# One diffusion-step kernel: the prompt's tile moved to the end of the projection, and three of the first expert's eight first-layer weight blocks multiplied in plain fp32

## The chip, the cores and the metric

One core of a Trainium2 chip runs the whole step. The metric is the device time of one execution in microseconds; before the change it is 2153.65 us, the median of three runs (2150.96 to 2155.9).

## The reference, cut to what matters

128 prompt rows and 1024 latent rows, both 1024 wide, go through one layer. All tensors are fp32.

```
hn   = rmsnorm(x) * (1 + scale1) + shift1            # modulation: silu(c) @ w_mod + b_mod
mix  = (gates * (pooling mixer, bidirectional RG-LRU)(hn @ w_in)) @ w_out
x    = x + gate1 * mix
hn   = rmsnorm(x) * (1 + scale2) + shift2
aff  = softmax(hn @ router_w)                        # 16 experts
gate, idx = top_k(aff over the rows, capacity)       # 128 latent rows and 16 prompt rows per expert
hid  = silu(hn[idx] @ w1) * (hn[idx] @ w3)           # 1024 -> 2048, per expert
y[idx] += (hid @ w2) * gate                          # 2048 -> 1024, per expert
out  = rmsnorm(x + gate2 * y)
```

Prompt and latent rows are routed separately, but an expert multiplies its 128 latent and 16 prompt rows together: 144 columns (`S`). Each expert has 24 MB of weights, so 384 MB are streamed once.

## The kernel before

The order on every engine is written out by hand: the program order of an engine is its issue order. Five stages follow one another.

1. **Start** (`norm1`, `mod_first`, `mod_second`, `hn_first`, `hn_cols`, `hn_low`, `dense_v`, lines 352 to 471). The 1152 rows are normed and transposed into `hn_hi` and `hn_lo`, while the first modulation columns come from 16 blocks `a` of `w_mod`. A matrix product in this kernel is split: a raw fp32 weight block is cast on ScalarE to `hi` (fp32r) and the rest is subtracted on VectorE to `lo` (`split`, lines 181 to 190), and three TensorE products hi·hi, hi·lo, lo·hi follow (`mm3`). Blocks `a` whose number is in `DP` are not split: they are multiplied by the 4-column `sil4` as plain fp32.
2. **Input projection, RG-LRU and pooling** (lines 702 to 830). The list `seq` says which 128 output columns come next; kinds `v`, `g2`, `g1`, `p`, `bp`, `bl` are dense products, `m` is a piece of the modulation (`mod_block`). `gates` uses five buffers of the tag `gate`; `softplus` is computed at the end of stage 1.
3. **Output projection, norm and routing** (lines 955 to 1241). `project(i, h)` computes half `h` of tile `i` (128 rows; tile 0 is the prompt, 1 to 8 the latents) with 24 matmuls of 512 columns, in the order of `steps`. VectorE multiplies by the gate row and adds into `x2s[i]` (lines 980 and 981). `norm2` squares on ScalarE, finishes the scale on VectorE (`go2`) and stores the normed rows. `router_a`, `router_b`, `router_c` give the router's logits. `pre`, `mids` and `post` hang the routing of earlier tiles on later steps: `mids[n]` holds pairs of a k at which a piece is put between the matmuls. `first_cols`, `first_row`, `first_rank`, `last_rank`, `list_hot` and `list_make` find the rank of each latent row for expert 0 and from it the list of its 128 rows. `prompt_a`, `prompt_b` and `prompt_c` pick the prompt rows of every expert. The prompt's tile stands second and fourth among the steps; the last step is (8, 1).
4. **Change over** (lines 1285 to 1354 and `first_x`). `gate2_to` multiplies the last two pieces of `w_mod` as plain fp32. `x_fetch` gathers rows from HBM by an indirect DMA of GpSimd, for the prompt from `hp_d` and for expert 0 from `hn_d`. The first weight blocks (`load_chunk`, 1 MB each) are loaded, one on SP before the last step has ended, the others from SP and ScalarE.
5. **Experts** (lines 1604 to 1712). A 128x4x512 block passes through five raw buffers, `split_hi` (ScalarE, fp32r) and `split_lo` (VectorE, bf16), and six buffers of halves. `products` first multiplies the hi parts of two blocks with 288 columns (x hi beside x lo), then the lo parts with 144 columns of bf16 x. `sums` adds the two halves of the accumulator. When `split_lo(n)` is issued, block n+5 is loaded. In expert 0, VectorE also runs `search`, ten rounds of a search for the other experts' thresholds, and hands a round to TensorE inside the products.

SP issues its DMAs in program order and waits at each for its operands.

Of the kernel before, what the change touches and what calls it, by code (L numbers as in the profile page):

```python
# [25 lines left out]
G0, G1, GX, G2 = 3, 8, 9, 15  # L26
FL, FM = 0, 0
DP = range(4)
# [21 lines left out]
def hybrid_step_kernel(ctx: ExitStack, tc: tile.TileContext, x_prompt, x_sample, state_lru, c, c_ctx,  # L50
# [23 lines left out]
    hp_d = dram.tile([SP, D], F32, name="hp_d")  # L74
# [46 lines left out]
    l_a = ini.tile([P, 16], F32, name="l_a")  # L121
    l_e = ini.tile([P, 16], F32, name="l_e")
    l_z = ini.tile([P, 16], F32, name="l_z")
    l_q = ini.tile([P, 16], F32, name="l_q")

    def softplus():
        A.activation(l_a, lamc, AF.Abs)
# [35 lines left out]
    s1 = const.tile([P, 2, KD], F32, name="s1")  # L163
# [131 lines left out]
    junk = xsp.tile([P, D], F32, name="junk")  # L295
    vsp = [[xsp.tile([P, 1024], F32R, name=f"v{n}{j}") for n in ("h", "l")] for j in range(2)]
# [141 lines left out]
    mod_first(3)  # L438
    mod_low(0)
    do_split(5)  # L440
# [3 lines left out]
    hn_first(0)  # L444
    do_split(8)

    for q in range(4):
        k = 2 * q
        if q < 3:
            do_split(4 * q + 10)  # L450
# [3 lines left out]
        hn_cols(k + 1)  # L454
# [4 lines left out]
        if q < 3:  # L459
            mod_low(q + 1)  # L460
            do_split(4 * q + 12 if q < 2 else HEAD + 2)
# [6 lines left out]
    softplus()  # L468
# [49 lines left out]
    def gates(j):  # L518
        vc, vhi, vlo, ghi, glo = LR[j]
        gt = []  # L520
        for m in range(4):
# [4 lines left out]
            r = lt.tile([P, LT], F32, name="gate", bufs=5)  # L526
# [24 lines left out]
    def scans(j):  # L551
# [11 lines left out]
        yl = lt.tile([P, T], F32R, name="yl", tag="gate", bufs=5)  # L563
# [45 lines left out]
    def pool_evac(g, a3):  # L609
# [50 lines left out]
    def mod_block(q, h, w):  # L660
# [6 lines left out]
        if h:  # L667
            mrow = mrp.tile([4, 256], F32, name="mrow", bufs=2)
            A.copy(mrow, t[:4, :256])
            later.append([5, lambda: mod_cols(1 + q // 8, 2 * (q % 8), 2, mrow)])  # L670
# [37 lines left out]
    conv(0)  # L708
    for j in range(2):
# [12 lines left out]
    for i in range(HEAD + 2, len(seq)):  # L722
        kind, j = seq[i]
        if kind == "m" and (kind, j) not in spl and i < done_split[0]:
            continue
        if (kind, j) != ("g1", 0):
            do_split(i + 4)
        for d in list(later):
            d[0] -= 1
            if d[0] <= 0:  # L730
                d[1]()
                later.remove(d)
        if kind == "bl" and j == 0:
            mg_hi = pool_sb["dp"].tile([P, KD, T], F32R, name="mg_hi", tag="D")
            mg_lo = big.tile([P, KD, T], F32R, name="mg_lo", tag="H2")
# [142 lines left out]
    g1r, mrows = [wo_g[:, KD * D:(KD + 1) * D].bitcast(F32), wop.tile([P, D], F32, name="g1r1")], {}  # L878
    for z in range(2):
        G.dma_start(g1r[z], row(z))  # L880
    x2s = {}
    for i in (1, 2):
        x2s[i] = sgp.tile([P, T], F32, name="sg")[:, :D]
        G.dma_start(x2s[i], x_rows(i))
# [9 lines left out]
    pgi = route.tile([P, 2], I32, name="pgi")  # L894
# [44 lines left out]
    def load_mrows(z):  # L939
        mrows[z] = [tk.tile([P, D], F32, name=f"s2r{z}", bufs=1),  # L940
                    tk.tile([P, D], F32, name="t2r", bufs=1) if z else rk.tile([P, D], F32, name="t2r0", tag="arow")]
        for n in range(2):
            SY.dma_start(mrows[z][n], row(2 + 2 * n + z))

    SY.dma_start(x2p, x_rows(0))
    load_mrows(1)
    load_mrows(0)

    def last_rows():
        x2s[8] = tk.tile([P, D], F32, name="x2l", tag="s2r0", bufs=1)  # L950
        SY.dma_start(x2s[8], x_rows(8))
# [3 lines left out]
    def project(i, h, mid=(), part=False):  # L955
        z = 1 if i else 0
        hs = slice(h * 512, (h + 1) * 512)
        if h == 0 and i not in x2s:
            x2s[i] = x2p if i == 0 else sgp.tile([P, T], F32, name="sg")[:, :D]
            if i:  # L960
                SY.dma_start(x2s[i], x_rows(i))
# [19 lines left out]
        V.tensor_tensor(x2s[i][:, hs], x2s[i][:, hs], tmp, op=OP.add)  # L981
# [12 lines left out]
    def norm2_b(i, n=1):  # L994
        z = 1 if i else 0
        x2, hn = x2s[i], hns[i]
        for q in range(n):
            s = slice(q * D // n, (q + 1) * D // n)
            V.scalar_tensor_tensor(hn[:, s], x2[:, s], rs2[:, i:i + 1], mrows[z][0][:, s], op0=OP.mult, op1=OP.mult)
            V.tensor_tensor(hn[:, s], hn[:, s], mrows[z][1][:, s], op=OP.add)  # L1000
        if z:
            SY.dma_start(x3_d[(i - 1) * P:i * P, :], x2)
        SY.dma_start(hn_d[(i - 1) * P:i * P, :] if i else hp_d[:, :], hn)
# [6 lines left out]
    def router_a(i):  # L1010
        hts[i] = tk.tile([P, KD, P], F32, name="ht", bufs=1)
        for h in range(2):
            t = tp_tile()
            for k in range(4):
                PE.transpose(t[:, k * P:(k + 1) * P], x2s[i][:, (4 * h + k) * P:(4 * h + k + 1) * P], ident)
            A.copy(hts[i][:, 4 * h:4 * h + 4, :], t.rearrange("p (a b) -> p a b", a=4))

    def router_b(i):
        z = 1 if i else 0
        t = tp_tile()  # L1020
        for k in range(KD):
            PE.matmul(t[:, :E], hts[i][:, k, :], rws[:, z, k, :], start=k == 0, stop=k == KD - 1)
        lts[i] = t
# [71 lines left out]
    def last_rank():  # L1095

        beat = first_rank(7, 0, 8, 1)
        t = tp_tile()
        for i in range(7):
            PE.matmul(t[:, i:i + 1], beat[:, i * P:(i + 1) * P], ones[:, 0:1], start=True, stop=True)  # L1100
        V.tensor_reduce(rank, wins, axis=AX.X, op=OP.add)
        V.tensor_tensor(rank[:, :7], rank[:, :7], t[:, :7], op=OP.subtract)

# [84 lines left out]
    def prompt_c():  # L1188
# [7 lines left out]
        V.tensor_copy(pgi, pgf)  # L1196
# [6 lines left out]
    steps = [(1, 0), (0, 0), (1, 1), (0, 1)] + [(i, h) for i in range(2, NT) for h in range(2)]  # L1203

    pre, mids, post = ([[] for _ in steps] for _ in range(3))
    n = 4
    for i in [1, 0] + list(range(2, NT - 1)):
        n = max(n + 1, 2 * i + 2)
        a, b = (4, KD - 1)
        mids[n].append((a, lambda i=i: router_a(i)))  # L1210
        mids[n].append((b, lambda i=i: (router_b(i), router_c(i))))
    pre[2].append(constants)
    pre[8].append(last_rows)
    pre[2].append(router_weights)
    mids[4].append((KD - 1, router_shift))
# [581 lines left out]
```

## Time and profile before

| what | us |
|---|---|
| median of three runs | 2153.65 |
| profiled execution | 2155.95 |
| its span, first to last instruction | 2154.2 |
| TensorE busy | 2070.4 |
| VectorE busy | 1709.6 |
| ScalarE busy | 1358.8 |
| stage 3 ends (last matmul of step (8, 1)) | 803.2 |
| first expert's first product | 832.6 |
| first expert's second layer starts | 906.7 |

Times inside the kernel are microseconds from the span's start. In a timeline a row is: start, time, engine, line, operation, output and inputs, count, and in brackets the idle time before it with what ended it. A matmul's time covers its way through the array, so that matmuls overlap: their pace is the distance of two starts. A plain fp32 matmul leaves two records.

### The profile page before, as it was taken

The page shows a single profiled execution, that of the slowest core. Times are in us where ns is not written, and L with a number is a line of the kernel's source. Part 1 is how long each engine was busy: PE and PEld are TensorE (multiplying, and loading weights), DVE is VectorE, ACT ScalarE, POOL GpSimd, SP SyncE. Part 2 cuts the span into 40 slices and gives each one's busy share as a digit, 9 for nine tenths or more (in the row PEclk, how much of TensorE's full clock was granted, in tenths as well). Part 3 has the DMA queues.
Part 4 walks back from the last instruction along what each step waited for, and adds up shares of the span by engine and source line. Part 5 has one row for each costly group of instructions (what it writes and reads, how often), then busy time and mean ns, then how long its engine had stood idle before and what let it go on. Part 6 is the DMA issues. An engine that isn't in the chain of part 4 may idle for free.

```text
span 2154.2 us, 40533 instructions
## 1 busy us (share of the span) xinstructions
PE 2070.4 (96%) x17269; PEld 1974.4 (92%) x17269; DVE 1709.6 (79%) x1847; ACT 1358.8 (63%) x1444; POOL 190.9 (9%) x324
## 2 busy tenths in 40 slices
PE   6999999999999987899999999999999999999995
PEld 4799998999998875899999999999999999999994
DVE  6788988732236467988988898998998998899896
ACT  6477675321112225677877777877877777777783
POOL 0000001010101001020010010011010011011021
PEclk9999999999999988999999999999999999999997
DMA  8133434174644238699999999999999999999995
GB/s 265 56 118 114 125 111 124 55 223 117 203 158 170 109 110 296 237 326 332 346 328 334 343 331 324 343 340 326 333 335 327 338 341 328 336 341 323 339 313 181
DMA packets 304820, 543.91 MB, mean 252 GB/s; under 512 B 16300, under 2 KB 85628, under 8 KB 304639
## 3 DMA queue, kind: packets, MB, share of 16 engines
q1 hardware_dynamic: 285306, 478.56, 64.0%
q0 software_dynamic: 15728, 52.77, 8.4%
q10 hardware_dynamic: 3604, 9.98, 1.4%
q8 instruction: 135, 2.21, 0.4%
q14 instruction: 47, 0.38, 0.1%
HBM read 500.60 MB, written 40.67 MB: 251 GB/s over the span
## 4 chain that ended last, share of the span: by engine, by line
PE 86%; DVE 8%; DMA 2%; ACT 2%; issue 1%; SPq 0%; DVEq 0%; ACTq 0%
PE ac L1465 37%; PE ac L1473 17%; PE a L198 6%; PE a L199 6%; PE a L200 6%; PE a L757 5%; DVE lo L1280 2%; PE a L984 1%; PE a L986 1%; PE a L985 1%; DMA xg<-hn_d,lgi 1%; PE tp L1404 1%; PE tp L1489 1%; DVE lo L189 1%; PE tp L665 1%
## 5 line engine op out<-in xcount | busy, mean ns | idle before, releaser
L1280 DVE TENSOR_TENSOR lo<-raw,hi 128x2048 bf16<-128x2048 f32 x384 | 870.9, 2281 | 0.0
L1274 ACT CAST hi<-raw 128x2048 fp32r<-128x2048 f32 x384 | 729.4, 1912 | 3.8 <-issue 2.2
L1465 PE MATMUL ac<-x,hi 128*128 128x288 f32 x4096 | 606.1, 300 | 0.0
L1465 PEld LDWEIGHTS ac<-x,hi 128*128 128x128 f32 x4096 | 553.0, 189 | 1.0 <-issue 0.9
L1473 PEld LDWEIGHTS <-lo 128*128 128x128 bf16 x6144 | 380.4, 98 | 36.7 <-DVE lo L1280 0.8
L1465 PE MATMUL ac<-hh,hi 128*128 128x288 f32 x2048 | 332.9, 304 | 0.0
L1478 ACT COPY bs<-ac 128x288 f32<-128x288 f32 x320 | 127.8, 399 | 290.6 <-PE ac L1473 289.1
L1473 PE MATMUL ac<-xb,lo 128*128 128x144 bf16 x4096 | 302.4, 227 | 0.6 <-DVE lo L1280 0.6
L1465 PEld LDWEIGHTS ac<-hh,hi 128*128 128x128 f32 x2048 | 279.9, 189 | 0.0
L198 PE MATMUL a<-hn_hi,hi 128*128 128x384 f32 x624 | 212.0, 340 | 0.0
L199 PE MATMUL a<-hn_lo,hi 128*128 128x384 f32 x624 | 210.8, 338 | 0.0
L200 PE MATMUL a<-hn_hi,lo 128*128 128x384 f32 x624 | 210.8, 338 | 0.0
L1473 PE MATMUL ac<-hb,lo 128*128 128x144 bf16 x2048 | 171.9, 227 | 0.0
L189 DVE TENSOR_TENSOR lo<-raw,hi 128x1024 fp32r<-128x1024 f32 (+1 forms) x76 | 86.7, 1163 | 78.8 <-ACT hi L188 78.2
L1479 DVE TENSOR_TENSOR h<-ac,bs 128x288 f32<-128x288 f32 x256 | 115.7, 452 | 42.1 <-ACT bs L1478 41.8
L198 PEld LDWEIGHTS a<-hn_hi,hi 128*128 128x128 f32 x624 | 117.1, 188 | 0.4
L199 PEld LDWEIGHTS a<-hn_lo,hi 128*128 128x128 f32 x624 | 117.2, 188 | 0.0
L200 PEld LDWEIGHTS a<-hn_hi,lo 128*128 128x128 f32 x624 | 117.2, 188 | 0.0
L1710 POOL TENSOR_TENSOR yps<-ot,modc 128x128 f32<-128x128 f32 x16 | 35.9, 2247 | 735.2 <-DVE ot L1479 735.2
L188 ACT CAST hi<-raw 128x1024 fp32r<-128x1024 f32 (+1 forms) x76 | 74.8, 1001 | 41.2 <-PE a L199 33.3
L1479 DVE TENSOR_TENSOR ot<-ac,bs 128x288 f32<-128x288 f32 x64 | 29.3, 457 | 69.7 <-ACT bs L1478 69.7
L699 ACT ACTIVATE sg<-a 128x1152 f32<-128x1152 f32 x16 | 18.1, 1134 | 82.4 <-PE a L200 82.3
(447 smaller groups left out, 2626.8 us busy)
## 6 DMA issues: line engine op xcount, KB each, us to landing
raw<-in_exp_w_dram SPq DMA_DIRECT2D x380, 1024.0 KB, 7.2
raw<-in_w_in_dram SPq DMA_DIRECT2D x28, 512.0 KB, 5.0
raw<-in_w_mod_dram SPq DMA_DIRECT2D x28, 512.0 KB, 5.3
araw<-in_w_mod_dram SPq DMA_DIRECT2D x18, 256.0 KB, 4.5
g_d<-sg ACTq DMA_DIRECT2D x8, 576.0 KB, 3.2
yh_d<-yh POOLq DMA_DIRECT2D x8, 576.0 KB, 3.1
yl_d<-yl POOLq DMA_DIRECT2D x8, 576.0 KB, 4.6
m_d<-sg POOLq DMA_DIRECT2D x8, 576.0 KB, 4.2
```

Of the source, the lines that this page charges most:

```text
L188: A.copy(h, raw)
L189: V.tensor_tensor(l, raw, h.bitcast(F32), op=OP.subtract)
L198: PE.matmul(out, whi, xhi, start=first, stop=False)
L199: PE.matmul(out, whi, xlo, start=False, stop=False)
L200: PE.matmul(out, wlo, xhi, start=False, stop=last)
L757: PE.matmul(a3[:, ch, :CH], w[:, k, :], y[:, k, cs], start=n == 0 and k == 0 and w is hi, stop=n == 1 and k == KD - 1 and w is ws[-1])
L1274: A.copy(hl[n][0], raw[n])
L1280: V.tensor_tensor(lo, r, hi.bitcast(F32), op=OP.subtract)
L1465: PE.matmul(a[:, r, :2 * S], w[0][:, k, c0 + r * P:c0 + (r + 1) * P], x2(kk), start=kk == first, stop=False)
L1473: PE.matmul(a[:, r, S:2 * S], w[1][:, k, c0 + r * P:c0 + (r + 1) * P], xb(kk), start=False, stop=kk == last)
L1478: A.copy(b, a[:, :, S:2 * S])
L1479: V.tensor_tensor(dst, a[:, :, :S], b, op=OP.add)
```

## The change

The diff is long; its parts, by number, with the core of each.

1. **Start.** Only three blocks `a` are plain. Splits are issued earlier, `mod_low` is one copy on ScalarE, and `hn_cols` is cut into `hn_mod` (VectorE, now ahead of the splits of its round) and `hn_high` (ScalarE). `softplus` moves behind the first `conv`.
2. **Stage 2.** Seven `gate` buffers instead of five; the next `m` piece is issued behind the evacuations of a `v` or `p` block (`sums_next`).
3. **Stage 3.** The prompt is last; the adds of tiles 1 to 7 go to GpSimd; `hp_d` and the prompt's stored rows are gone.
4. **Change over.** The prompt's norm, routing and top-k run here, and its columns come from a product of `x2p` with a one-hot matrix (`pick`) instead of a gather. All five raw buffers are filled as soon as they are free.
5. **Expert 0.** Blocks 2, 3, 6, 7, 10, 11 stay raw and are multiplied with the unsplit `xf0` of 144 columns.

```
-DP = range(4)
+DP = range(3)
...
-            r = lt.tile([P, LT], F32, name="gate", bufs=5)
+            r = lt.tile([P, LT], F32, name="gate", bufs=7)
...
     for q in range(4):
         k = 2 * q
-        if q < 3:
-            do_split(4 * q + 10)
+        if q:
+            hn_mod(k + 1)
+        do_split(4 * q + 10 if q < 3 else HEAD + 2)
         dense_v(0, k)
...
-        hn_cols(k + 1)
+        hn_high(k + 1)
         dense_v(1, k)
...
-        V.tensor_tensor(x2s[i][:, hs], x2s[i][:, hs], tmp, op=OP.add)
+        (G if 0 < i < NT - 1 else V).tensor_tensor(x2s[i][:, hs], x2s[i][:, hs], tmp, op=OP.add)
...
-    steps = [(1, 0), (0, 0), (1, 1), (0, 1)] + [(i, h) for i in range(2, NT) for h in range(2)]
+    steps = [(1, 0), (2, 0), (1, 1), (2, 1)] + [(i, h) for i in list(range(3, NT)) + [0] for h in range(2)]
...
+    for i, n in zip(range(1, 8), (5, 6, 7, 8, 10, 12, 14)):
+        mids[n] += routed(i)
...
+    post[13] += [lambda: part_ranks(4, 6, 0, 6, 1)]
+    pre[15] += [lambda: affinities(7, 8), lambda: first_cols(6, 7), root]
+    mids[15].append((5, lambda: router_a(8, 0)))
+    mids[15].append((KD - 1, lambda: first_row(6, 7)))
+    post[15] += [lambda: norm2_a(8), lambda: part_ranks(0, 4, 6, 7, 4), lambda: go2(slice(8, 9), (0,)),
+                 lambda: A.activation(ready[:, 0:1], ready[:, 1:2], AF.Exp), lambda: first_rank(6, 0, 7, 1, (0,)),
+                 lambda: go2(slice(8, 9), (1,)), lambda: norm2_b(8)]
+    mids[16] += [(2, lambda: router_a(8, 1)),
+                 (6, lambda: (router_b(8), router_c(8), affinities(8, 9), first_cols(7, 8), root(),
+                              part_ranks(4, 6, 6, 7, 4), first_rank(6, 0, 7, 1, (1, 2))))]
...
+    mids[17] += [(1, lambda: (first_row(7, 8), value_parts(6, 8), last_rank(0))),
+                 (4, lambda: router_a(0, 0)),
+                 (6, lambda: (last_rank(1), hot0.append(list_hot(rk, V, 0, rank)), router_b(0, range(4))))]
...
+    prompt_square(1)
+    router_a(0, 1)
+    V.tensor_tensor(ss2[:, 0:1], sq2[:, 0:1], sq2[:, 1:2], op=OP.add)
+    go2(slice(0, 1), (0,))
+    A.activation(ready[:, 0:1], ready[:, 1:2], AF.Exp)
+    list_make(rk, 0, hot0[0])
+    router_b(0, range(4, KD))
+    go2(slice(0, 1), (1,))
+    router_c(0)
...
+    PLAIN = ((0, 1), (1, 1), (2, 1))
+    plain = [4 * fb + 2 * w + i for fb, w in PLAIN for i in range(2)]
...
+    def load_next(n):
+
+        free.add(n)
+        while todo[0] < RB or todo[0] - RB in free:
+            load_chunk(todo[0])
+            todo[0] += 1
...
     xg = x_fetch(hn_d[:, :], lgi[:, 0:1])
-    ahead(1, 0)
+    gate2_to(3)
+    affinities(0, 1)
+    prompt_a()
+    gate2_to(10)
+    ahead(1, 1)
+    prompt_b()
+    prompt_c()
+    gate2_to(13)
...
+    prompt_pick(0)
+    lows(1)
+    ahead(2, 2)
+    xf0 = ep.tile([P, KD, S], F32, name="xf")
+    xq = xf0[:, :, CAP:]
+    prompt_rest = prompt_cols(0, xq)
+    gate2_to(NGT * KD)
...
+    def plain_products(a, ns, c0, x):
+        for r in range(2):
+            for i, n in enumerate(ns):
+                for k in range(4):
+                    PE.matmul(a[:, r, :S], raw[n][:, k, c0 + r * P:c0 + (r + 1) * P], x[:, 4 * i + k, :],
+                              start=i == k == 0, stop=i == 1 and k == 3)
...
                     a = acc_pair()
+                    if base in plain:
+                        if (fb, w, q) not in SKIP:
+                            next(find, None)
+                        plain_products(a, (base, base + 1), q * 256, xf0)
+                        A.copy(h[:, 2 * q:2 * q + 2], a[:, :, :S])
+                        continue
...
+                    if (e, fb, w, q) == (0, 0, 0, 0):
+                        V.tensor_tensor(grow[:, gs], gp[:2].rearrange("p a b -> p (a b)")[:, gs], brow[:, gs], op=OP.add)
...
+                    if base + i in plain:
+                        del raw[base + i]
+                        load_next(base + i)
```

For the second half of the experts, expert 7 now builds the prompt's columns with `prompt_pick(1)` and `prompt_cols(1)()`: eight plain fp32 matmuls and eight ScalarE copies instead of a gather and eight transposes.

## Rows read from the trace of the kernel before

**Rows 1.** The page, busy time: engine, busy us, share of the span, instructions.
```profile
PE 2070.4 (96%) x17269; PEld 1974.4 (92%) x17269; DVE 1709.6 (79%) x1847; ACT 1358.8 (63%) x1444; POOL 190.9 (9%) x324
```

**Rows 2.** Windows: stretch, length, busy us (instructions) per engine, granted clock, DMA share, GB/s.
```profile
762.00:803.20 41.20, 37.05 (x158) 30.11 (x157) 24.88 (x87) 10.89 (x18) 2.28 (x5) 0.79 0.25 90
803.20:832.60 29.40, 17.26 (x92) 8.85 (x90) 18.55 (x52) 12.46 (x21) 11.38 (x11) 0.77 0.84 296
832.60:906.70 74.10, 61.95 (x678) 59.89 (x677) 70.78 (x96) 46.36 (x46) 0.00 (x0) 0.95 0.74 254
906.70:987.60 80.90, 79.14 (x804) 76.64 (x801) 72.81 (x65) 61.24 (x60) 11.40 (x6) 1.00 0.94 326
```

**Rows 3.** Waits of PE: who waited for whom, us in total, times, longest.
```profile
PE tp L1374 <- DVE msk L1367: 10.3, 6, 2.5
PE tp L1446 <- DMA xg<-hn_d,lgi: 7.3, 1, 7.3
...
PE a L199 <- DVE hn_lo L368: 2.6, 4, 1.0
...
PE a L198 <- ACT gate L527: 1.5, 1, 1.5
```

**Rows 4.** Timeline of PE, end of stage 3 to the first expert's first product.
```profile
762.00 0.39 PE L984 MATMUL a<-wo_g,mg_hi 128*128 128x512 f32 x1
...
779.20 1.19 PE L1092 MATMUL tp<-ident,cols 128*128 128x128 f32 x4 [3.44 <-DVE cols L1081]
...
803.15 0.38 PE L1092 MATMUL tp<-ident,col 128*128 128x128 f32 x2
...
832.62 2.46 PE L1465 MATMUL ac<-x,hi 128*128 128x288 f32 x16
```

**Rows 5.** Timeline of the DMA queue of SP, step (7, 0) of stage 3.
```profile
772.41 0.32 SPq L1003 DMA_DIRECT2D hn_d<-hn  x1
772.84 0.37 SPq L961 DMA_DIRECT2D sg<-in_x_sample_dram  x1
```

**Rows 6.** Timeline of DVE, steps (7, 0) to the change over.
```profile
765.79 0.28 DVE L1178 MAX8 pval<-pa 16x8 f32<-16x128 f32 x1
...
768.46 0.13 DVE L151 TENSOR_SCALAR rv_b<-ss 128x1 f32<-128x1 f32 x1
...
776.81 0.69 DVE L981 TENSOR_TENSOR sg<-sg,tmp 128x512 f32<-128x512 f32 x1 [3.68 <-issue]
...
807.37 1.03 DVE L156 TENSOR_TENSOR rq_b<-rq_b,rv_b 128x1 f32<-128x1 f32 x1
```

**Rows 7.** Timeline of POOL, change over.
```profile
806.03 2.35 POOL L1324 TENSOR_TENSOR hn<-x2l,s2r 128x1024 f32<-128x1024 f32 x1 [24.66 <-ACT hn L992]
...
809.88 2.48 POOL L1343 TENSOR_TENSOR hn<-hn,t2r 128x512 f32<-128x512 f32 x2 [0.25 <-ACT hn L1331]
```

**Rows 8.** The chain that ended last: start, time, what.
```profile
819.61 10.06 DMA xg<-hn_d,lgi
```

**Rows 9.** Timeline of PE in expert 0: one pair of split products, and the next.
```profile
903.49 2.36 PE L1465 MATMUL ac<-x,hi 128*128 128x288 f32 x16
...
906.66 1.30 PE L1465 MATMUL ac<-hh,hi 128*128 128x288 f32 x8
```

**Rows 10.** Plain fp32 in the trace: timeline of PE, then one line's min, median, max ns.
```profile
20.61 3.60 PE L386 MATMUL tp<-araw,sil 128*4 128x512 f32 x8
...
752.93 1.05 PE L1092 MATMUL tp<-ident,cols 128*128 128x128 f32 x8
...
L1092 PEld LDWEIGHTS tp<-ident,cols x12: 188/192/333, 752.7 to 779.8; 128*128 128x128 f32 x12
```

**Rows 11.** Timeline of DVE in expert 0: splits, and one round of the search.
```profile
833.61 6.67 DVE L1280 TENSOR_TENSOR lo<-raw,hi 128x2048 bf16<-128x2048 f32 x3
...
842.78 0.25 DVE L1375 SCALAR_TENSOR_TENSOR met<-tp,cand 128x112 f32<-128x112 f32 x1
...
844.88 0.45 DVE L1479 TENSOR_TENSOR h<-ac,bs 128x288 f32<-128x288 f32 x1
```

More of the change, by code (lines that the diff above doesn't have):

```diff
@@ L120, in hybrid_step_kernel @@
     pk = const.tile([P, 16], F32, name="pk")
[L121 to L124, printed above, removed]
     def softplus():
+        scratch = lt.tile([P, LT], F32, name="gate", bufs=7)
+        l_a, l_e, l_z, l_q = (scratch[:, 16 * n:16 * n + 16] for n in range(4))
         A.activation(l_a, lamc, AF.Abs)
@@ L721, in hybrid_step_kernel, with turn_later @@
             scans(0)
[L722 to L727, printed above, removed]
+    def turn_later():
         for d in list(later):
@@ L732, in hybrid_step_kernel, with sums_next @@
                 later.remove(d)
+    def sums_next(n):
+        while n and seq[at[0] + 1][0] == "m":
+            at[0] += 1
+            m = seq[at[0]][1]
+            do_split(at[0] + 1)
+            turn_later()
+            mod_block(m // 2, m % 2, spl.pop(("m", m)))
+            if m == 31 - 2 * NGT:
+                later.append([5, mod_rows])
+            n -= 1
+    at = [HEAD + 1]
+    while at[0] + 1 < len(seq):
+        at[0] += 1
+        i = at[0]
+        kind, j = seq[i]
+        if (kind, j) != ("g1", 0):
+            do_split(i + 4)
+        if kind == "m":
+            turn_later()
         if kind == "bl" and j == 0:
@@ L937, in router_shift @@
         A.copy(lsh, t[:, :2 * E].rearrange("p (z e) -> p z e", z=2))
[L939 to L943, printed above, removed]
[L945 to L951 removed]
+    x2s[2] = tk.tile([P, D], F32, name="x2e", bufs=1)
+    SY.dma_start(x2s[2], x_rows(2))
+    mrows = []
+    for n in range(2):
+        mrows.append(tk.tile([P, D], F32, name=f"mr{n}", bufs=1))
+        SY.dma_start(mrows[n], row(3 + 2 * n))
+    SY.dma_start(x2p, x_rows(0))
     pss = {}
@@ L1008, in norm2, with router_a, router_b @@
         norm2_b(i)
[L1010 to L1018, printed above, removed]
+    def router_a(i, h):
+        if h == 0:
+            hts[i] = tk.tile([P, KD, P], F32, name="ht", bufs=1)
+        t = tp_tile()
+        for k in range(4):
+            PE.transpose(t[:, k * P:(k + 1) * P], x2s[i][:, (4 * h + k) * P:(4 * h + k + 1) * P], ident)
+        A.copy(hts[i][:, 4 * h:4 * h + 4, :], t.rearrange("p (a b) -> p a b", a=4))
+    def router_b(i, ks=range(KD)):
         z = 1 if i else 0
[L1020 to L1023, printed above, removed]
+        if i not in lts:
+            lts[i] = tp_tile() if i else acc2.tile([P, 512], F32, name="a2")
+        for k in ks:
+            PE.matmul(lts[i][:, :E], hts[i][:, k, :], rws[:, z, k, :], start=k == 0, stop=k == KD - 1)
     def router_c(i):
@@ new lines, in hybrid_step_kernel @@
+    steps = [(1, 0), (2, 0), (1, 1), (2, 1)] + [(i, h) for i in list(range(3, NT)) + [0] for h in range(2)]
+    pre, mids, post = ([[] for _ in steps] for _ in range(3))
+    for i, n in zip(range(1, 8), (5, 6, 7, 8, 10, 12, 14)):
+        mids[n] += routed(i)
+    pre[2] += [constants, router_weights]
+    mids[4].append((KD - 1, router_shift))
+    pre[9] += [lambda: affinities(1, 5), lambda: first_cols(0, 4), root]
+    mids[10].append((6, lambda: first_row(0, 4)))
+    pre[11] += [lambda: part_ranks(0, 4, 0, 4, 1)]
@@ L1269, in load_chunk @@
             raw[n] = r
+    todo, free = [0], set()
+    def load_next(n):
[3 more added lines that the diff above has]
+            todo[0] += 1
     def split_hi(n):
-        if n < NC:
+        if n < NC and n not in plain:
             hl[n] = (ew.tile([P, 4, 512], F32R, name="hi", bufs=HB), ew.tile([P, 4, 512], BF16, name="lo", bufs=HB))
@@ L1276, in split_lo @@
     def split_lo(n):
-        if 0 <= n < NC:
+        if 0 <= n < NC and n not in plain:
             hi, lo = hl[n]
```

214 lines of the change are left out of this document (93 added, 121 removed).

## The prediction

> **What bounds the kernel now.** I read four views, in this order. The page first: TensorE is busy for 96% of the span [rows 1], so only places where it stands still, runs at its low clock, or does work that can go are worth anything. The windows then say where. From 762.0 to 803.2 TensorE is idle for 4.1 us and its mean clock is 0.79. From there to the first expert's first product it is busy for 17.3 of 29.4 us. Through expert 0's first layers it is busy for 62.0 of 74.1 us while VectorE is busy for 70.8. After that it loses 1.8 us in 81 [rows 2]. The list of waits says for whom: expert 0 waits for the search on VectorE (10.3 us in six waits) and once, 7.3 us, for the gathered rows of expert 0; the other waits that this change touches are 2.6 us in stage 1 and 1.5 us in stage 2 [rows 3]. The timelines give the sizes of the pieces. So the end is set by TensorE, and what precedes the experts moves the end one for one: the weight stream is at 0.94 of its engines in the settled experts but only at 0.74 in expert 0 and 0.25 at the end of stage 3 [rows 2].
>
> **The change part by part.** Times are in the profiled execution (2155.95 us, 2.3 above the median of the runs).
>
> *A, stage 1.* Doing `hn_mod` ahead of the splits lets `hn_high` and the splits run side by side; the waits of `dense_v` for `hn_low` are 2.6 us in four [rows 3]. Block `a3` goes from two plain matmuls to four split ones. Eight records of plain 512-column work take 3.60 us [rows 10], so the block costs 1.8 us plain and, at the pace of a split matmul, about half of that; its cast and subtraction stand where both engines wait for the transposes. I take -2 us; from -5 (some of the start's clock loss goes too) to +2 (a split comes late).
>
> *B, stage 2.* With seven gate buffers the first evacuations of block 7 needn't wait for the scans of block 6, which is the 1.5 us wait [rows 3]; `softplus` moves to where TensorE has a dense product to do; the `m` pieces fill places where the pooling is awaited. -2 us; from -6 to +2, since one mod row buffer instead of two can add a wait of the same kind.
>
> *C, from step 14 to the first product.* Through step 13 both orders hold 14 steps and six tiles' routers, so I start both at 762.0 [rows 4]; the new one has four transposes of `first_row(4, 6)` more, 0.4 us. A step is 24 matmuls in 5.5 us, a router 2.6 us.
>  - Step (8, 0) with tile 7's router: 8.1 us. In step (8, 1) TensorE stops at `router_a(8, 0)`, as the load of x's tile 8 is behind the store of tile 7's normed rows in SP's queue. That is the pattern that stands before, there for tile 7: store at 772.4, load 772.8, VectorE's add held 3.7 us until 776.8, TensorE held 3.4 us until 779.2 [rows 4 to 6]. For tile 8 the store comes some 8.3 us after step 13 (three us of `part_ranks` stand ahead of it on VectorE), the row lands 4 us later, and the wait is 1.5 us. Step (8, 1) ends at 762.4 + 8.1 + 7.6 = 778.1.
>  - Tile 8's list now runs beside the prompt's two steps (11 us). On VectorE: mult and add 1.4, ranks 1.5 and 1.1, scale 1.2, normed rows 2.5, logits 0.3, affinities 1.6, column 0.2: 9.8 us before `first_row(7, 8)`, which TensorE reaches after 7.4. So it waits 2.5 us, and a spell at the low clock, as the windows have behind the earlier stops, costs some 2.5 more. The last projection ends 18.5 us after 778.1, at 796.6, instead of 803.2.
>  - From there the prompt's chain: add 1.8, square and transposes 1.6, list of expert 0 and scale 1.5, router and logits 1.6, affinities 1.6, `prompt_a` 0.8, `prompt_b` 2.7 on VectorE (765.8 to 768.5) [rows 6], seven `gate2` matmuls on TensorE ahead of `prompt_c` (3 to 5), `prompt_c` 2, pick 2, eight matmuls of `prompt_cols` 2 to 4 (0.26 each at the high clock [rows 10]), its scaling and split 1.7, transposes of the latent rows 1: about 23 us. The gather for expert 0 is issued some 4 us into this and takes 10 [rows 8], so the prompt is late now, not the gather. First product at 819.6 instead of 832.6 [rows 4]: -13 us.
>  - Bounds: if every hand-over is as quick as the sum of the durations and no clock is lost, it is at 811, -22; if gate2, low clock and VectorE's queue all lie end to end, the 23 are 39 and it is +3.
>
> The adds on GpSimd speak against this part. A half tile takes GpSimd 1.24 us [rows 7] instead of VectorE's 0.69 [rows 6], and beside such an instruction a one-column VectorE operation took 1.03 us [rows 6, 7], six times its neighbours' 0.16. [...]
>
> *D, expert 0.* A pair of blocks in one half (16 hi, 16 lo matmuls) takes 3.17 us, 903.49 to 906.66 [rows 9], or 0.199 us for hi and lo of one weight tile. A plain matmul of 128 columns takes 0.26 us [rows 10]; 512 columns take 0.90, so 144 scale to 0.25. I take 0.25: 96 of them, 24.0 us for 19.1 before, +4.9 on TensorE. VectorE loses six splits of 2.2 us and six adds of 0.45 [rows 11], 16 us. TensorE's work in the phase is then 62.0 + 4.9, about 67 with the search's own matmuls, and VectorE's 70.8 - 16 = 55 plus the last input splits: the phase becomes TensorE's. The waits for the search (10.3) fall to about 3, because beside plain blocks a search round (2.1 us, 842.78 to 844.88 [rows 11]) has no split in front of it. Against this stands the accumulator that `gp` holds until behind the first `sums`: the second product waits 2 us. Removed: waits 7 and 6 of other splits' lateness; added: 4.9 and 2: -6 us. A raw buffer is now held until the plain product has ended, and blocks are loaded in order, so blocks 7, 11 and 15 each come only one block ahead of their use; with 3.1 us per load this just holds. Bounds: -14 (all 12 us of idle go and VectorE's relief lasts) to +18 (plain matmuls at 0.44, load and product one after the other; or the loads late by 5 us three times).
>
> *E, expert 7.* Eight plain matmuls instead of eight transposes: +1 us (0 to 3). The gather's queue no longer matters.
>
> Sum: -2 -2 -13 -6 +1 = -22 us; 2134 for the profiled execution, **2132** against the median.
>
> **Rivals.**
>  1. *More than that.* The prompt's chain overlaps the gate2 work and VectorE is free in expert 0: C at -20, D at -11, total about -35, 2118. For it: VectorE's share of 70.8 in 74.1. Against: C has some 25 hand-overs.
>  2. *A new wait takes the old one's place.* The prompt's chain replaces the gather's wait fully (C at -3) while D keeps -6 and A and B their -4: -12, 2142. For it: the gather is 10 us and hidden at no cost, the chain is twice that.
>  3. *The transfer decides.* The raw buffers held by plain blocks starve the first expert and the stream gives back what was won: C's 13 are lost as waits for blocks, 2148 to 2156. For it: the stream is at 0.94 in settled experts [rows 2], so a lost lead is regained slowly. Against: five blocks now load during the prompt's chain, where only one or two did.
>  4. *Slower.* A 4-byte weight load isn't hidden. Its record is 188 ns [rows 10] and a plain matmul makes two; with two passes of 120 ns, all in series, a matmul takes 0.62 us, and 96 of them cost 40 us more than split: 2132 + 96 x 0.37 = 2168. It decides from 0.52 us a matmul on. Against it: four matmuls of `first_row` in 1.05 us [rows 10], which leaves no room for serial loads. [...]
>
> **How the numbers follow.** My forecast, 2120 to 2141, has 0.53; rival 1 (below 2120) 0.13; rival 2 (2141 to 2149) 0.18; rival 3 (2149 to 2158) 0.09; rival 4 (above) 0.07. The range 2113 to 2149 leaves out rivals 3 and 4 and the far end of rival 1. A change of 0.2% is 4.3 us, about what can be told from none: faster 0.84, same 0.09, slower 0.07.
>
> **What would show it.** C: the first product of 288 columns near 820; TensorE waiting in the change over for the prompt's column work and not for `xg`; a wait at `router_a(8, 0)` and one at `first_row(7, 8)`. D: records of the plain product at a pace of 0.12 to 0.13 us, second layer starting some 68 us after the first product, VectorE no longer the busiest; settled experts still 79 us apart. A and B: stage 3's step 13 ending near 758. The prediction is wrong if the plain pace is far above 0.25 us a matmul, if TensorE waits for raw blocks in expert 0, or if the distance from the last projection to the first product isn't between 17 and 30 us.

## The result and the profile after

The changed kernel takes **2138.5 us** (median of four runs, 2137.2 to 2139.92), 6.5 more than the 2132.0 forecast. The kernel before took 2152.31 beside it (2150.39 to 2155.9); the ratio is 0.9934, interval 0.9917 to 0.9951, so 10.5 to 17.9 us were won. The profiled execution took 2137.2 us, its span 2135.4. That is 18.8 below the span of before, more than the 13.8 between the medians: the profile before is the slowest of its four runs, that of after the fastest. All stretches below are from these two.

| stretch | before | after | difference | forecast |
|---|---|---|---|---|
| start to the end of step 13 (A, B) | 762.0 | 755.0 | -7.0 | -4 |
| step 14 to the first product (C) | 70.6 | 53.7 | -16.9 | -13 |
| first product to second layer of expert 0 (D) | 74.0 | 74.5 | +0.5 | -6 |
| second layer of expert 0 to the end (E) | 1247.5 | 1252.2 | +4.7 | +1 |
| span | 2154.2 | 2135.4 | -18.8 | -22 |

So what precedes the experts won more than forecast, and the experts, which should have won 5, lost 5. Some 4 us of C's difference can be those of one execution of before: e2 (below) has the same code up to the end of stage 3, and its trace takes 36.5 us at a clock of 0.91 where [rows 2] have 41.2 at 0.79, and 66.6 us from step 14 to the first product. Against that, C won 12.9.
```profile
763.08:799.55 36.47, 32.43 (x157) 26.57 (x156) 24.47 (x87) 10.78 (x18) 2.28 (x5) 0.91 0.27 98
```
The page after, busy time (columns as in [rows 1]):
```profile
PE 2062.9 (97%) x17287; PEld 1969.8 (92%) x17287; DVE 1687.1 (79%) x1831; ACT 1356.2 (64%) x1457; POOL 195.5 (9%) x331
```
The windows after, cut at the same events as [rows 2]:
```profile
755.00:786.60 31.60, 29.96 (x168) 24.58 (x166) 23.62 (x76) 13.58 (x25) 4.99 (x11) 1.00 0.22 84
786.60:808.70 22.10, 17.66 (x87) 9.71 (x86) 11.21 (x42) 9.04 (x16) 1.07 (x1) 0.77 0.95 337
808.70:883.20 74.50, 64.68 (x676) 62.27 (x677) 57.74 (x87) 39.68 (x50) 0.00 (x0) 0.98 0.75 259
883.20:962.20 79.00, 78.22 (x789) 75.72 (x787) 71.86 (x65) 60.98 (x60) 11.40 (x6) 1.00 0.95 333
```
The first line has one stop left (1.49 us) and no low clock (0.79 before, 1.00 now, 41.2 us become 31.6). The second shows the raw buffers being filled during the prompt's chain (DMA share 0.95). In the third, VectorE went from 70.8 busy us to 57.7 and is no longer the busiest, as forecast, and yet the stretch is as long as before: TensorE is idle for 9.8 of its 74.5 us. The waits of TensorE say for whom (whole run; as [rows 3]):
```profile
PE tp L1432 <- DVE msk L1425: 6.1, 3, 2.7
PE tp L1388 <- DVE oh L1386: 3.7, 1, 3.7
...
PE tp L1442 <- DVE gt L1437: 2.1, 1, 2.1
PE a L194 <- DVE hn_lo L366: 1.9, 1, 1.9
...
PE ac L1513 <- ACT xp L1403: 1.2, 1, 1.2
...
PE ac L1343 <- DMA hi<-in_w_mod_dram: 0.9, 1, 0.9
...
PE tp L1462 <- DMA xg<-hn_d,lgi: 0.8, 1, 0.8
```
The 7.3 us for the gathered rows are gone (0.8 is another expert's gather). The search still costs 6.1 us, now in three waits, and there is a wait that the kernel before did not have: `oh`, the one-hot of `prompt_pick`. The timeline of TensorE after puts the pieces in place (as [rows 4]; `L1432` is the search's matmul, `L1528` the plain product):
```profile
755.00 0.39 PE L994 MATMUL a<-wo_g,mg_hi 128*128 128x512 f32 x1
...
768.95 0.63 PE L1021 MATMUL tp<-ident,sg 128*128 128x128 f32 x4 [1.49 <-DVE mx L1042]
...
780.21 0.41 PE L1098 MATMUL tp<-ident,col 128*128 128x128 f32 x2
...
788.36 1.09 PE L1021 MATMUL tp<-ident,x2p 128*128 128x128 f32 x4 [1.60 <-DVE x2p L991]
...
803.28 2.05 PE L1395 MATMUL ac<-pick,x2p 128*128 128x128 f32 x16 [0.46 <-ACT pick L1389]
...
808.70 2.45 PE L1513 MATMUL ac<-x,hi 128*128 128x288 f32 x16 [0.96 <-DVE x L1486]
...
816.21 1.16 PE L1521 MATMUL ac<-xb,lo 128*128 128x144 bf16 x16
820.05 0.57 PE L1432 MATMUL tp<-msk,ones 128*128 128x112 bf16 x8 [2.67 <-DVE msk L1425]
820.45 4.15 PE L1528 MATMUL ac<-xf,raw 128*128 128x144 f32 x32
...
860.90 4.15 PE L1528 MATMUL ac<-xf,raw 128*128 128x144 f32 x32
864.79 2.38 PE L1513 MATMUL ac<-x,hi 128*128 128x288 f32 x16
```
Read from it: the wait at `router_a(8, 0)` (768.95) is there, none at `first_row(7, 8)` (780.21); the first product comes at 808.70; a plain product of 16 matmuls takes 864.79 - 860.90 = 3.89 us, 0.243 each; and ahead of the first one TensorE stands for 2.67 us at the search's matmul. The other two such waits are 1.76 us (837.73) and 1.65 us (855.83), each again at the first product of a plain half (a half is two blocks: one group of 512 columns of `w1` or `w3`; the plain ones are three groups of `w3`). VectorE's timeline shows what the first of them waits for:
```profile
815.66 2.29 DVE L1327 TENSOR_TENSOR lo<-raw,hi 128x2048 bf16<-128x2048 f32 x1 [0.77 <-ACT hi L1321]
817.87 0.27 DVE L1433 SCALAR_TENSOR_TENSOR met<-tp,cand 128x112 f32<-128x112 f32 x1
...
818.90 1.09 DVE L1425 TENSOR_TENSOR msk<-lg,cand 128x896 bf16<-128x896 f32 x1
```
TensorE had finished the round before at about 816.4 (a row of 0.57 us at 815.80), but on VectorE a split stands in front (815.66 to 817.87), and the round takes 2 us itself. TensorE, which has a round at the *start* of a plain product, gets there with nothing else to do.

### The profile page after: what moved, and what is told of

The parts are those of the page before. It is cut to its first block, busy times and chain, and to the rows that moved or that the text cites. A ratio compares the mean times of both kernels' runs of the same rounds, so it can differ in the third digit from the quotient of the medians.

```text
span 2135.4 us, 40544 instructions
## 1 busy us (share of the span) xinstructions
PE 2062.9 (97%) x17287; PEld 1969.8 (92%) x17287; DVE 1687.1 (79%) x1831; ACT 1356.2 (64%) x1457; POOL 195.5 (9%) x331
## 4 chain that ended last, share of the span: by engine, by line
PE 88%; DVE 7%; ACT 3%; DMA 1%; issue 1%; SPq 0%; POOL 0%; DVEq 0%; ACTq 0%; POOLq 0%
PE ac L1513 37%; PE ac L1521 17%; PE a L194 6%; PE a L195 6%; PE a L193 6%; PE a L776 5%; DVE lo L1327 1%; PE a L994 1%; PE a L996 1%; PE a L995 1%; PE tp L665 1%; PE tp L1462 1%; PE tp L1544 1%; PE tp L666 1%; PE ac L1528 1%
## 5 line engine op out<-in xcount | busy, mean ns | idle before, releaser
L1327 DVE TENSOR_TENSOR lo<-raw,hi 128x2048 bf16<-128x2048 f32 x378 | 857.6, 2282 | 3.0 <-ACT hi L1321 3.0
L1321 ACT CAST hi<-raw 128x2048 fp32r<-128x2048 f32 x378 | 718.4, 1914 | 5.5 <-DMA raw<-in_exp_w_dram 5.5
L1513 PE MATMUL ac<-x,hi 128*128 128x288 f32 x4000 | 591.7, 300 | 2.1 <-ACT xp L1403 1.2
L1513 PEld LDWEIGHTS ac<-x,hi 128*128 128x128 f32 x4000 | 539.8, 188 | 2.7 <-ACT xp L1403 1.3
L1521 PEld LDWEIGHTS <-lo 128*128 128x128 bf16 x6048 | 373.3, 98 | 36.2 <-DVE lo L1327 0.3
L1521 PE MATMUL ac<-xb,lo 128*128 128x144 bf16 x4000 | 294.2, 227 | 0.1
L1534 DVE TENSOR_TENSOR ot<-ac,bs 128x288 f32<-128x288 f32 x64 | 29.3, 457 | 67.4 <-ACT bs L1533 67.4
```

The source lines that it names most:

```text
L1321: A.copy(hl[n][0], raw[n])
L1327: V.tensor_tensor(lo, r, hi.bitcast(F32), op=OP.subtract)
L1513: PE.matmul(a[:, r, :2 * S], w[0][:, k, c0 + r * P:c0 + (r + 1) * P], x2(kk), start=kk == first, stop=False)
L1521: PE.matmul(a[:, r, S:2 * S], w[1][:, k, c0 + r * P:c0 + (r + 1) * P], xb(kk), start=False, stop=kk == last)
L1534: V.tensor_tensor(dst, a[:, :, :S], b, op=OP.add)
```

## The experiments

Each kernel is the changed one with one edit, unless said; `M` or `P` in an expectation are its theories. The changed kernel was measured in two sets, 2138.5 us and 2139.0 (below); differences are to 2138.8 between them. The kernel before ran beside all.

| run | median us | runs | ratio to before, interval | to the change |
|---|---|---|---|---|
| e1 no plain blocks | 2139.14 | 5 | 0.9947, 0.9933 to 0.996 | +0.3 |
| e2 before, with plain blocks | 2154.74 | 11 | 1.0009, 1.0 to 1.0018 | |
| e3 rounds in the middle | 2133.13 | 5 | 0.9913, 0.9899 to 0.9927 | -5.7 |
| e4 one-hot earlier | 2132.65 | 5 | 0.9915, 0.9901 to 0.9928 | -6.1 |
| e5 adds on VectorE | 2145.28 | 6 | 0.9968, 0.9956 to 0.9979 | +6.5 |
| e6 five gate buffers | 2140.39 | 6 | 0.9947, 0.9935 to 0.9959 | +1.6 |
| e7 hn_mod late | 2143.26 | 6 | 0.9958, 0.9946 to 0.997 | +4.5 |
| e8 three edits | 2126.45 | 4 | 0.9879, 0.9865 to 0.9894 | -12.3 |
| e9 the change again | 2139.03 | 6 | 0.994, 0.9927 to 0.9954 | |
| e10 e4, no plain blocks | 2135.40 | 6 | 0.9922, 0.9909 to 0.9935 | -3.4 |
| e11 e3 and e4 | 2126.87 | 4 | 0.9884, 0.9867 to 0.9901 | -11.9 |
| e12 e11, four halves plain | 2126.58 | 4 | 0.9879, 0.9862 to 0.9896 | -12.2 |

### What the plain blocks are worth

```
-    PLAIN = ((0, 1), (1, 1), (2, 1))
+    PLAIN = ()
```


> The changed kernel with all of expert 0's blocks split again (the prompt stays last). Theory M: the plain blocks cost TensorE 4.7 us and take 16 us from VectorE, which without them is the busiest again; expert 0's first layers then take 76 to 78 us instead of 74.5, and the time is 2 to 3 us above the changed kernel's 2138.5, about 2141. Rival R: in the changed kernel nothing hangs on VectorE's splits, the plain blocks are only a cost: 4 to 5 us below, about 2134.

e1: 0.3 us slower by the medians; by the ratios 1.5 us slower than e9, with intervals that overlap. As they stand in the change, the three plain halves move the time by nothing that these runs can tell: M's loss of 2 to 3 us is not excluded, R's gain of 4 to 5 is. The stretch in its trace (first product to second layer):
```profile
808.30:885.58 77.28, 64.20 (x677) 61.93 (x677) 72.41 (x99) 50.35 (x56) 0.00 (x0) 0.91 0.74 251
```
Against the change's third window VectorE has 14.7 us more and the stretch is 2.8 us longer; TensorE's mean clock is 0.91.

In e2 the same three halves are plain in the kernel before, with its order of loads and its prompt in second place:
```
+    PLAIN = ((0, 1), (1, 1), (2, 1))
...
-        if n < NC:
+        if n < NC and n not in plain:
...
+                    if base in plain:
+                        if (fb, w, q) not in SKIP:
+                            next(find, None)
+                        plain_products(a, (base, base + 1), q * 256, xf0)
```


> The kernel before with the same three blocks of expert 0 in plain fp32, nothing else changed. Theory M: VectorE bounds expert 0 there (70.8 of 74.1 us busy), so taking 16 us from it and adding 4.7 to TensorE shortens the phase by 1 to 5 us: 2147 to 2151 against 2152.3. Rival R (the plain blocks are only a cost): 4 to 5 us above the kernel before, about 2157.

Its interval is 0 to 3.9 us slower than before: not the gain of the one theory, and at most the lower part of the other's loss. TensorE waits 7.6 us in three for `msk`, all at the start of a plain half, instead of 10.3 in six [rows 3]. In its trace the stretch takes 78.6 us (829.68 to 908.25) instead of 74.0, and two of the stops, 3.08 and 2.88 us, are followed by plain products of 5.82 and 5.53 us instead of 4.15. So the pattern is the same in both kernels, which points at the place of the search round and not at the change over.

### The search round in the middle of a plain product

```
     def plain_products(a, ns, c0, x, step=None):
         for r in range(2):
...
+            if step is not None:
+                step(r)
...
-                        if (fb, w, q) not in SKIP:
-                            next(find, None)
-                        plain_products(a, (base, base + 1), q * 256, xf0)
+                        plain_products(a, (base, base + 1), q * 256, xf0,
+                                       (lambda r: None if r else next(find, None)) if (fb, w, q) not in SKIP else None)
```


> The changed kernel with the search's round inside a plain product (after its first 8 columns of matmuls per half, the first r) instead of ahead of it. Theory M: the three waits at the plain blocks' start (2.67, 1.76 and 1.65 us, for msk behind a split on VectorE) are hidden by 1.95 us of plain matmuls each: 4 to 6 us below the changed kernel, 2133 to 2134.5. Rival L: TensorE then waits for the next thing in line (the raw blocks' loads or the ScalarE copy): within 1.5 us of 2138.5.

5.7 us faster. Its timeline of TensorE, same place as 820.05 above:
```profile
817.85 2.17 PE L1528 MATMUL ac<-xf,raw 128*128 128x144 f32 x16
820.68 0.55 PE L1432 MATMUL tp<-msk,ones 128*128 128x112 bf16 x8 [0.67 <-DVE msk L1425]
821.07 4.15 PE L1528 MATMUL ac<-xf,raw 128*128 128x144 f32 x32
```
and its window from first product to second layer:
```profile
809.34:877.50 68.16, 63.67 (x677) 61.47 (x677) 57.77 (x87) 39.73 (x50) 0.00 (x0) 1.00 0.79 276
```
Eight of the sixteen plain matmuls now cover the split and the round on VectorE; the waits for `msk` fall from 6.1 to 1.1 us, the clock is 1.00 (0.98 in the change), and the stretch is 68.2 us: the number that the prediction had for the change itself, though not by its terms (see D below).

### Expert 7's one-hot one half earlier

`prompt_pick(1)` is cut into `prompt_hot` (one VectorE instruction) and the rest.
```
+                if e == 7 and (fb, w) == (1, 1):
+                    oh1 = prompt_hot(1)
                 if e == 7 and (fb, w) == (2, 0):
-                    prompt_pick(1)
+                    prompt_pick(oh1)
```


> The changed kernel with expert 7's one-hot matrix computed one block earlier, its transposition left in place. Theory M: the 3.67 us that TensorE waits there for VectorE's one-hot are gone and nothing else moves: 3 to 4 us below, about 2135. Rival L: the wait moves to the transposition's copy or to the column products: within 1 us of 2138.5.

6.1 us faster, more than expected. What it removes, in the change's timelines of VectorE
```profile
1417.51 2.28 DVE L1327 TENSOR_TENSOR lo<-raw,hi 128x2048 bf16<-128x2048 f32 x1
1419.71 0.28 DVE L1386 TENSOR_SCALAR oh<-iof,pgf 128x128 f32<-128x128 f32 x1
```
and of TensorE:
```profile
1415.20 1.17 PE L1521 MATMUL ac<-xb,lo 128*128 128x144 bf16 x16
1420.04 0.47 PE L1388 MATMUL tp<-ident,oh 128*128 128x128 f32 x1 [3.67 <-DVE oh L1386]
1420.17 3.55 PE L1513 MATMUL ac<-x,hi 128*128 128x288 f32 x16
1423.56 1.17 PE L1521 MATMUL ac<-xb,lo 128*128 128x144 bf16 x16
1424.53 2.36 PE L1513 MATMUL ac<-x,hi 128*128 128x288 f32 x16
```
An instruction of 0.28 us is issued behind two sums and two splits on a VectorE that works without a gap, and TensorE stands 3.67 us, in the settled experts where nothing else hides it. The product behind the stop then takes 3.55 us instead of 2.36. With the edit the stretch from expert 0's second layer to the end is 2130.4 - 883.4 = 1247.0 us, as before the change (1247.5), and in e9, which has the stop again, 2137.4 - 883.1 = 1254.3: all of the +4.7 was this.

### Stage 3, stage 1 and stage 2

```
-        (G if 0 < i < NT - 1 else V).tensor_tensor(x2s[i][:, hs], x2s[i][:, hs], tmp, op=OP.add)
+        V.tensor_tensor(x2s[i][:, hs], x2s[i][:, hs], tmp, op=OP.add)
```


> The changed kernel with tiles 1 to 7's adds back on VectorE (14 adds of 0.69 us there instead of 1.29 on GpSimd). Theory P (the adds on GpSimd pay because VectorE needn't wait for x's rows): VectorE is held by the load of a tile's rows in stage 3 as in the kernel before, TensorE stops at the column transposes of the ranks: 2 to 6 us above 2138.5. [...]

6.5 us slower, the first product 5.9 us later (814.57). The wait of TensorE that appears in stage 3, from its list of waits:
```profile
PE tp L1098 <- DVE cols L1087: 4.7, 1, 4.7
```
and VectorE's timeline there:
```profile
748.77 0.68 DVE L990 TENSOR_TENSOR tmp<-a,g1r 128x512 f32<-128x512 f32 x1
753.21 0.69 DVE L991 TENSOR_TENSOR sg<-sg,tmp 128x512 f32<-128x512 f32 x1 [3.76 <-DMA sg<-in_x_sample_dram]
...
755.17 0.29 DVE L1087 COPY cols<-lg 128x256 f32<-128x256 f32 x1
```
With the add on VectorE, the wait for tile 7's row of x (3.76 us) stands in front of everything that VectorE still has to do for the tiles before, and TensorE wants the last of it. In the change the same add waits in GpSimd's queue (timelines of SP and POOL), and nothing that TensorE needs is behind it:
```profile
748.92 0.37 SPq L971 DMA_DIRECT2D sg<-in_x_sample_dram  x1
752.95 1.29 POOL L991 TENSOR_TENSOR sg<-sg,tmp 128x512 f32<-128x512 f32 x1 [9.69 <-ACT arow L1099]
```
The row names ScalarE's `arow`, which was done at 752.79; that the load holds the add is read from the times: the add starts 4.0 us after the load's issue, as in e5 (749.16 and 753.21). It is the wait of [rows 4 to 6] (3.68 us on VectorE, 3.44 on TensorE), and what took it out of the change is the engine of the add; the prompt's new place, which e5 has too, doesn't do it. Of a cost that the adds on GpSimd bring to VectorE the traces show next to nothing: one VectorE instruction (`L1124`, 756.99), beside an add of GpSimd from 755.97 to 757.26, took 0.42 us instead of e5's 0.35.

```
-            r = lt.tile([P, LT], F32, name="gate", bufs=7)
+            r = lt.tile([P, LT], F32, name="gate", bufs=5)
```
(and the two other tiles of that tag)

> The changed kernel with five gate buffers instead of seven. Theory B: the 1.5 us wait of block 7's gates for the scans of block 6 comes back, with some clock loss: 1.5 to 4 us above 2138.5. Rival: the other moves of stage 2 removed it already: within 1 us.

1.6 us slower, with intervals that overlap; not settled by the times. Its stage 2 takes 578.5 us, that of the change 577.2 and 577.5 (e9), and its trace has a wait that the change's has not, which supports a gain of 1 to 1.6 us:
```profile
PE a L193 <- ACT gate L526: 2.4, 1, 2.4
```

```
     for q in range(4):
         k = 2 * q
-        if q:
-            hn_mod(k + 1)
...
         dense_v(0, k)
...
+        hn_mod(k + 1)
         hn_high(k + 1)
```
(and the call for k = 1 ahead of the loop)

> The changed kernel with VectorE's modulation of the odd column blocks behind the splits again, as in the kernel before. Theory A: stage 1's waits for hn_low come back, four times about 0.7 us: 2 to 4 us above 2138.5. Rival: stage 1's gain is that of the earlier splits and of the split block a3: within 1 us.

4.5 us slower, and the first product comes 4.9 us later (813.58). The waits of TensorE in stage 1:
```profile
PE a L193 <- ACT hn_hi L353: 2.8, 1, 2.8
PE a L194 <- DVE hn_lo L366: 2.3, 4, 0.9
```
The change has no wait for `hn_hi` from that line (L353), and one for `hn_lo` of 1.9; and over the first 100 us the mean granted clock is 0.95 here and 0.97 there.

### Together

e8 has e3's and e4's edits and moves gate2's last three products behind the transposes of expert 0's rows.
```
     prompt_rest = prompt_cols(0, xq)
-    gate2_to(NGT * KD)
...
+        gate2_to(NGT * KD)
         for f in low:
```


> The changed kernel with e3's and e4's edits, and the last three gate2 products behind the transposes of expert 0's rows instead of ahead of them. Theory M: 5 + 3.7 us of the first two and 1 to 1.4 us of the third add up: 2127 to 2130. Rival L (waits move on): 2134 to 2138.

12.3 us faster than the change, 26 than the kernel before. To see whether the third edit has a part in it, and what the plain halves are worth once the rounds are in their middle, four more ran side by side. e9 has no edit, e11 leaves the third edit out:

> The changed kernel once more, without an edit, as the base for the three beside it. Both theories: 2137 to 2140 us, first product at 808.7 us, expert 0's first layers 74.5 us long, the 3.7 us wait for `oh` in expert 7 there again.

> The search round in the middle of each plain product and expert 7's one-hot a block earlier, gate2 as in the change. Theory W: the two add, -4 to -6 each, so 2127 to 2130 us; the first layers take 68 us at a clock of 1.00, and the third edit of the run with three fixes (gate2's last three products moved) was worth nothing. Rival H (moving gate2's products won something): 2130 to 2133 us.

2139.03 and 2126.87: the two edits add up, and the third is worth nothing that can be measured (2126.45 with it). e10 is e4's edit and `PLAIN = ()`:

> Expert 7's one-hot a block earlier, and no plain block in expert 0 (all eight halves split). Theory W (the plain blocks pay, but the search rounds at their starts hide it): the first layers take 77.3 us as in the run without plain blocks, against 68.2 us with plain blocks and rounds in their middle, and the weight stream gives nothing back, so this is 7 to 10 us slower than the run with both fixes and 2 us slower to 2 us faster than the change without the pick's edit would be less 5: 2133 to 2136 us. Rival G (the stream sets the pace, what a plain block wins is given back later): within 3 us of the run with both fixes.

2135.4 against e11's 2126.87, 8.5 us. So the plain halves pay 8.5 us with the round in their middle, where they paid 0 to 3 with it at their start (e1 against e9, and e10 against e4: 2.8), and the weight stream does not give it back. VectorE's relief is not all of the 8.5. Some 5.4 us stand at expert 0's second product (timeline of TensorE in e10, then ScalarE's in e10 and in the change):
```profile
816.90 4.21 PE L1515 MATMUL ac<-x,hi 128*128 128x288 f32 x16 [4.76 <-ACT xp L1405]
...
822.82 2.36 PE L1515 MATMUL ac<-x,hi 128*128 128x288 f32 x16
```
```profile
810.31 3.73 ACT L1321 CAST hi<-raw 128x2048 fp32r<-128x2048 f32 x2
813.91 2.93 ACT L1405 ACTIVATE xp<-ac,modcol 128x128 f32<-128x128 f32 x8
```
```profile
810.59 2.94 ACT L1403 ACTIVATE xp<-ac,modcol 128x128 f32<-128x128 f32 x8
```
`xp` is `prompt_rest`, whose eight ScalarE copies free the accumulator. In e10 the casts of blocks 2 and 3 stand in front of them on ScalarE, and TensorE waits 4.76 us for them instead of the change's 1.16 and then takes 4.21 us instead of 2.36; plain blocks have no cast. Whether the split blocks would do as well with `prompt_rest` issued ahead of those casts was not run. e12 takes the fourth half too:
```
-    PLAIN = ((0, 1), (1, 1), (2, 1))
+    PLAIN = ((0, 1), (1, 1), (2, 1), (3, 1))
```
(and the search's last rounds, which hang on that half, are issued in its branch)

> As the run with both fixes, and the fourth half (blocks 14 and 15) plain too. Theory W: with three halves plain TensorE is busy for 63.7 of 68.2 us, so there are at most 1 us of search waits left to win, while 32 plain matmuls at 0.243 us cost 1.4 us more than split ones at 0.199; 0 to +2 us against the run with both fixes. Rival V (VectorE still decides, at 57.8 of 68.2 us, and each half taken from it pays): -2 to -4 us.

2126.58, no difference to e11. VectorE is relieved once more, to 54.3 us in a stretch of 67.4 (68.0 in e11), so in this stretch it no longer decides:
```profile
807.86:875.23 67.37, 65.04 (x677) 62.99 (x677) 54.28 (x84) 34.59 (x47) 0.00 (x0) 1.00 0.76 261
```
Behind the stretch TensorE waits 3.20 us for expert 1's gathered rows in this trace, 1.15 in e11's, which takes more than the 0.7 back (the profiled execution of e12 is the slowest of its four). e11, with two edits, is the version to keep; e8 and e12 can't be told from it.

## Why the prediction was right and where not

The total came out inside the forecast's own band (2120 to 2141) in part by luck: in the two traces A to C won 6.9 us more than forecast and D and E 10.2 less.

**A and B** were right in sign and too small: -7.0 for -4. Stage 1, to the last matmul of `dense_v`, went from 85.55 to 82.08 us, -3.5 for -2. The waits for `hn_lo`, which the prediction named, fell only from 2.6 to 1.9; those for `hn_hi` fell from 4.1 to 1.7. `hn_mod` ahead of the splits alone is worth 4.5 (e7); without it stage 1 takes 86.7 us, longer than before, so its other parts cost something. Stage 2 won 4.0, but hardly by the mechanism that was forecast (windows of it before and after):
```profile
85.55:666.73 581.18, 573.66 (x3316) 568.41 (x3316) 366.69 (x403) 267.10 (x282) 32.24 (x115) 1.00 0.44 132
82.08:659.26 577.18, 568.63 (x3316) 562.44 (x3316) 368.98 (x413) 269.00 (x284) 32.27 (x115) 0.99 0.45 135
```
TensorE is idle for 8.6 us of it instead of 7.5: the `gate` wait of 1.5 is gone, but others are new or longer. It is busy for 5.0 us less with as many matmuls; the 128x384 ones of the dense products take 336 ns on average instead of 338 to 340. e9 has this too (568.6 us busy) and e2 has it not (573.9); no run tests why. The gate buffers fit with 1 to 1.6 (e6, overlapping intervals).

**C** has the forecast's mechanism in its pieces. Steps (8, 0) and (8, 1) took 15.95 us (755.00 to 770.95) for 16.1, with the wait at `router_a(8, 0)` of 1.49 us for 1.5 and for the reason given: the load of x's tile 8 stands behind a store in SP's queue, and VectorE's add is held for it (timelines of SP and VectorE).
```profile
763.59 0.32 SPq L1009 DMA_DIRECT2D hn_d<-hn  x1
764.01 0.37 SPq L971 DMA_DIRECT2D sg<-in_x_sample_dram  x1
```
```profile
768.16 0.69 DVE L991 TENSOR_TENSOR sg<-sg,tmp 128x512 f32<-128x512 f32 x1 [3.85 <-issue]
```
The prompt's chain took 22.1 us for 23, with the waits where they were put (`x2p`, `pick`, x's columns) and none for `xg`; 0.94 us for a block of `w_mod` was not in the sum. What did not come are the 2.5 us of waiting at `first_row(7, 8)` and 2.5 us of low clock behind it: the prompt's two steps took 15.7 us for 18.5. VectorE's list, summed at 9.8 us, was done in time.

One term was put at nothing without a reason: the stop of tile 7, which before lies in this stretch (779.20 [rows 4]). In the new order it would fall into step 13, where e5 has it, with 102.6 us from stage 3's first matmul to step 14 instead of 95.7. The prediction starts both kernels at 762.0 as if it were gone, and what removes it are the adds on GpSimd, which were booked as a risk: e5 shows them as a gain of 6.5 us. What they cost VectorE in the trace is 0.07 us on one instruction (above). What decided was whose queue holds the wait for a DMA. No run puts the prompt back in its old place with the rest kept, so what its place alone is worth is read from the traces and not shown by an experiment.

**D** is the step that failed: "The waits for the search (10.3) fall to about 3, because beside plain blocks a search round (2.1 us, 842.78 to 844.88 [rows 11]) has no split in front of it." The blocks that follow the plain ones are split beside them, so a split of 2.29 us does stand in front (815.66), and the round was put at the start of the plain product, where TensorE has nothing left to do. The three waits of 2.67, 1.76 and 1.65 us stand there, and e3 takes away 5.0 of their 6.1 us by moving the round by eight matmuls. The sum had a second fault: it removes 7 us of waits for the search and 6 of other lateness, but TensorE was idle for only 12.1 us before, 10.3 of them for the search [rows 3], so less than 2 were left. Without the 6, its own terms give 74.1 - 7 + 4.9 + 2 = 74.0 for the measured 74.5, and that by terms that miss both ways: the waits for the search fell by 4.2, TensorE's work grew by 2.7, and the accumulator cost 1.2. So the 68.2 us of e3 don't confirm the sum either: they are 63.7 of work and 4.5 of waits, where the prediction's terms were 67 and about 5. What held: 0.243 us a matmul for 0.25, VectorE's 57.7 for 55, no wait of TensorE for a block's load.

**E** counted eight matmuls for eight transposes and left out the VectorE instruction that feeds them. The term of +1 was +4.7: 3.67 us of waiting for `oh` and some 1.2 us (3.55 for 2.36) of slower matmuls behind it; e4 takes all of it away. In the trace `oh` starts at 1419.71, as the split ahead of it on VectorE (2.28 us from 1417.51) ends. Asking what stands ahead of an added instruction on its queue, as was done for stage 3, would have found both D's and E's waits.

Of the rivals, the first had C at -20, which nearly came, and D at -11, which did not. The second has come nearest in time (2142), but not at its place: the prompt's chain did not replace the gather's wait, the experts' new waits did. The third (blocks late) and the fourth (weight loads not hidden) are refuted: TensorE's list has no wait for the load of a weight block, what E lost comes back with e4, and 0.243 us is far from 0.52.

## What to carry to other kernels

When work is taken off a busy engine, look again at the instructions that others wait for on it: a hand-over that sat inside a long product is exposed when it is moved to the start of the next one. Put the hand-over in the middle of the consumer's own work, and a one-hot or another small operand a block early; here both cost nothing and gave 12 us. An edit whose gain is hidden by a wait looks worthless until the wait is gone: the plain halves measured 0 to 3 us in the change and 8.5 behind e3's and e4's edits. A wait for a DMA belongs in the queue of the engine that has nothing urgent behind it; here that gave 6.5 us (e5).

## What the runs showed of the hardware

Some of TensorE's stops cost more than their length. Behind 4.76 us of standing (e10, 816.90) sixteen matmuls of 288 columns took 4.21 us instead of 2.36; over 809 to 877 the mean granted clock is 0.92 in e10 and 1.00 in e11, whose stop at the same place is 1.16 us. Behind 3.67 us (the change, expert 7) they took 3.55, with a clock of 0.69 over 1420.00 to 1424.50. Behind 2.67 us (the change, 820.05) the plain product took the same 4.15 as the undisturbed one at 860.90. In these rows the length of a stop alone does not decide it. In e2 a plain product took 5.53 us behind a stop of 2.88. In the change, the wait of 2.08 us for `gt` and 64 matmuls of 16 columns were followed by a clock of 0.84 (872.80 to 883.20); in e3, which has the same matmuls behind a wait of 2.13 us, the mean over the whole stretch is 1.00 (809.34 to 877.50). In e1, with a stop of 4.76 us, it is 0.91 (808.30 to 885.58).
